# One fp32 matmul per span on a half of TensorE's columns, in batches, in place of three fp32r matmuls

## The chip, the cores and the metric

The kernel runs on one core of one Trainium2 chip. What counts is the time of one execution on the device, in microseconds: the median of three runs.

## What is computed

One layer of a mixer for a prompt of 1024 tokens and for one new token of each of 8 samples. The parts that matter here are the attention outputs of the prompt, cut to their core:

```python
def nsa_core(...):                  # for a block of queries
    ...                             # o_c: attention over compressed keys; imp: importance of blocks
    _, idx = lax.top_k(imp, n_sel)  # blocks of 64 keys that a query selects
    s_s = jnp.where(m_s, s_s, NEG)  # scores of the selected keys, causal
    p_s = jax.nn.softmax(s_s, axis=-1)
    o_s = jnp.einsum('bqgrnl,bgqnld->bqgrd', p_s, v_sel)
    ...
    p_w = jax.nn.softmax(jnp.where(m_w, s_w, NEG), axis=-1)   # the last 512 keys
    o_w = jnp.einsum('bqgrk,bkgd->bqgrd', p_w, vw)
    return o_c, o_s, o_w

o_a = gw[..., 0] * o_c + gw[..., 1] * o_s + gw[..., 2] * o_w  # gates by query and head
```

There are 8 query heads in 2 groups; the 4 heads of a group share keys and values of 64 channels. Everything else (modulation, projections, the spatial mix, gates, merge, output projection) surrounds this.

## The kernel before

The work comes in stages: modulation and projections of the tokens (to some 250 us of the profiled span), attention of the samples (to 410 us), attention of the prompt (some 415 to 822 us), merge and output projection (to the end). Beside the attention of the samples and of the prompt run channel-major projections as filler: `stream(jobs)`, whose matmuls write `mm` banks. A job has three pieces (344 columns each) of 24 matmuls; `paced()` lets the jobs last as long as the attention and keeps a rest of them, PACE_REST pieces, for the time after it.

All order is fixed when the program is made. Each stream of work is a Python generator; `Plan` estimates when each engine gets to what has been emitted, from a cost for each operation, and `Plan.go` always takes the next step of the stream that would make PE wait least. The result is one list of instructions for each engine, which the engine works off in order, with semaphores where one engine needs what another made. A wrong estimate changes the order, not what is computed.

Most matmuls are fp32r, one pass; a number is split into a high and a low half where more precision is needed, and three products of halves are added up. A matmul on plain fp32 operands is also possible; it shows in the trace as two instructions.

The attention of the prompt goes over 16 tiles (`TILES`: two groups, eight tiles of 128 queries each). `front` prepares a tile's queries, the compressed branch, the selection and the maxima of the scores. A tile has spans (`spans(i)`): pairs of a branch (1 the window, 0 the chosen blocks) and a tile of 128 keys, 2 to 13 of them, 132 in all 16 tiles. For each span:

- `scores` makes the scores, keys by (head, query), 128 x 512, with two matmuls into an `st` bank, and `pt` = exp of them on ScalarE; on the diagonal and at the window's far edge GpSimd sets entries to zero (`affine_select`, 40 of them). There are four `pt` buffers.
- `low` makes the halves of p: `p2[:, 0]` by a copy on ScalarE or (each third span) VectorE, `p2[:, 1]` by a subtraction on VectorE or (each third) GpSimd.
- `outputs` has three matmuls for it into a `pv` bank. `vv` holds, for each tile of keys, [v_hi, ones, v_lo] of 64 columns each, so the first and the third have 128 columns, of which 64 give the sums of p, and the second has 64 columns:

```python
pe.matmul(x, lhsT=v[:, 0:128], rhs=p2[:, 0], start=first, ...)
pe.matmul(x[0:64], lhsT=v[:, 128:192], rhs=p2[:, 0], start=False, ...)
pe.matmul(x, lhsT=v[:, 0:128], rhs=p2[:, 1], start=False, ...)
```

The window's spans come first and fill one bank, then the chosen ones fill another. When a branch is done, `weigh` copies the row of sums (`sr`) and the outputs (`u`) out of the bank on ScalarE and spreads the sums over partitions by a DMA (`s8`). When both are done, `close` forms the weights gate / sum, sends them through DRAM (`w_d`) to be spread over partitions (`f`), multiplies `u` by them on GpSimd, adds the compressed branch (two matmuls, `vc4` by `pgT`) and stores the tile. Closing the last tile of a group lets what depends on it go on; closing the last of all ends the stage. DMAs are issued from SP's queue, in order.

In the profile nearly every instruction has the line L217, that of the helper that records operations, so groups are told apart by their tiles: `pv<-p,vv` are the output matmuls, `p<-pt` and `p<-pt,p` the halves, `u`, `sr`, `s`, `f` what `weigh` and `close` handle, `mm<-hh,c0h` and the like the jobs, `mm<-araw,cT` the fp32 matmuls of the modulation (9 x 512), `mx<-plT,wck` another fp32 one.

Of the kernel before, what the change touches and what calls it, by code (L numbers as in the profile page):

```python
# [24 lines left out]
EPS = 1e-6  # L25
# [3 lines left out]
class Pack:  # L29
    """Constants that depend on the shapes alone, as columns of one [128, n] array."""  # L30
# [62 lines left out]
class Plan:  # L93
    """Estimates when the engines get to what has been emitted, so that independent streams of work can be
    emitted in an order in which the engines wait little. It has no part in what is computed."""
# [35 lines left out]
    def meet(x, y):  # L131
        """Whether two accesses to a tile, as box() gives them, overlap."""
# [8 lines left out]
    def after(self, ap, writes_only, engine=None):  # L141
        """When the accesses to the elements of ap are over."""
# [117 lines left out]
def nsa_gmlp_step(ctx: ExitStack, tc: tile.TileContext, a: dict):  # L260
# [46 lines left out]
    def rows(name, n, m=128):  # L307
        """The n elements of an input on each of m partitions."""
# [38 lines left out]
    def rsqrt(out, x, scale, n, p=128):  # L347
        """out = (x * scale + EPS) ** -0.5"""
# [24 lines left out]
    def weights(todo):  # L373
        """Loads slices (key, source, columns) in order and cuts them into hi and lo, but for those used as they are."""
# [46 lines left out]
    def x_turned(first):  # L421
        """RMS-normalised x, transposed: every other tile."""
# [26 lines left out]
    def x_loads():  # L449
        """The tiles of x behind the weights of the modulation, which all wait for."""  # L450
# [38 lines left out]
    def modulation():  # L489
        """Shift and scale of the samples and the prompt (column 8), and from them h."""  # L490
# [54 lines left out]
    def h_split():  # L545
        """h as its halves, as it comes."""
# [27 lines left out]
    def rope_tab(which):  # L574
        """[cos * g | sin * g'] so that rope(x * g) = x * cos_g + swap(x) * sin_g"""
# [9 lines left out]
    def constants():  # L585
        """What P1 needs beside its weights, each in time."""
# [25 lines left out]
    def fold(i, p, n):  # L612
        """The rows of the hi and lo halves of the samples, added."""
# [12 lines left out]
    def norm_rope(p, m, i, nh, t, final, done, x=None):  # L626
        """rope(rms_norm(p) * g) into the parts of final: (first head, end, out)"""
# [85 lines left out]
    def gate_rows():  # L713
        """The gate rows of the modulation, to DRAM until the end."""
# [137 lines left out]
    class Chunk:  # L852
        """128 columns of a weight as hi and lo [128, k, 128]."""
# [17 lines left out]
    def paced():  # L871
        """Whether the jobs are not ahead of the attention, so that they last as long as it does."""
# [8 lines left out]
    SPANS, PACE_LEAD, PACE_FRONT, PACE_REST = 132, 12, 14, 6  # L881
# [18 lines left out]
    def stream(jobs):  # L900
        """Jobs of (source of weights, body, condition): the weights of the next job load while this one runs."""
# [24 lines left out]
    def gate_tanh(p, n):  # L926
        """tanh(p / 2), so that p * sigmoid(p) = p * (1 + tanh(p / 2)) / 2"""
# [24 lines left out]
    def z_body(br, c):  # L952
        """silu(z) of a branch, times x where that is there, to DRAM until the merge."""
# [13 lines left out]
    def products(br):  # L967
        """What the projection of a branch takes, as its halves."""
# [23 lines left out]
    def gate_job(br, c):  # L992
        """tanh of half the merge gates of 128 channels, to DRAM until the merge."""
# [14 lines left out]
    def merge_job(br, j):  # L1008
        """Two chunks of 128 channels of a branch in model width, times the gate: all of m, or added to it."""
# [44 lines left out]
    def hand_over():  # L1054
        """When the rotary parts are done, their space goes to the weights of the jobs."""
# [50 lines left out]
    def decode():  # L1106
# [3 lines left out]
        def gather(name, s):  # L1110
            """Rows of sample s: partition p holds its tokens 8p..8p+7."""
# [5 lines left out]
        def window(src, dst, newrow, s):  # L1117
            """The last 511 cached rows and the new one: partition p holds rows 4p..4p+3."""
# [17 lines left out]
        def window_out(what, s):  # L1136
            """The window of a sample when it is loaded; it goes to its output."""
# [19 lines left out]
        def windows():  # L1157
            """The windows in turn, each when there is room, so that the other loads don't wait behind it."""
# [16 lines left out]
        # queries [hi | lo], by sample in zero-padded columns  # L1175
# [21 lines left out]
        # gates by (sample, head)  # L1197
# [9 lines left out]
        # compressed rows and key scores  # L1207
# [51 lines left out]
        def window_keys():  # L1259
            """Scores of the window and the compressed values, beside the selection."""  # L1260
# [19 lines left out]
        # compressed keys  # L1280
# [13 lines left out]
        def fold2(out, b):  # L1294
            """Rows of the hi and lo queries, added."""
# [3 lines left out]
        def softmax(x, mcol, gcol):  # L1299
            """Raw scores to probabilities, times the gate if there is one"""  # L1300
# [34 lines left out]
        # scores of the selected blocks and the new row  # L1335
# [14 lines left out]
        def turn_p(x, n, name):  # L1350
            """Probabilities [64, n*128] to [128, n, hi 64 | lo 64]"""
# [34 lines left out]
        # values of the selected and window rows, two samples at a time  # L1386
# [49 lines left out]
        for par in range(2):  # L1436
# [12 lines left out]
    areg = region("a", "right")  # L1449
    TILES = [(0, i) for i in (1, 2, 3, 4, 0, 5, 6, 7)] + [(1, i) for i in (2, 3, 4, 5, 6, 1, 7, 0)]  # L1450
    L1, L2, vv = ({(g, w): areg.tile(shape, FR, name=f"{n}{g}{w}") for g, w in ((0, 0), (0, 1), (1, 0))}
                  for n, shape in (("L1", [128, T]), ("L2", [96, T]), ("vv", [128, 8, 192])))
    for x in (L1, L2, vv):
        x[1, 1] = x[0, 1]
    PT_BUFS, P_BUFS = 4, 4
# [3 lines left out]
    one = areg.tile([128, 64], F32, name="one")  # L1459
# [14 lines left out]
    def g_load(j):  # L1474
        """Gates of a tile by (branch, head, token), eight on a partition."""
# [8 lines left out]
    def prepare():  # L1484
        for n in range(2):
            k_load(n)
        for n in range(PT_BUFS):
            e_load()
# [37 lines left out]
    def blocks():  # L1526
        """The rows of L2 that take the maxima to the keys of their blocks."""
# [6 lines left out]
    def keys():  # L1534
        """L1 = [k_hi; k_hi], L2 = [k_lo; blocks] and [v_hi | v_lo] of the branches of the groups, three at a time."""
        for g, w in ((0, 1), (0, 0), (1, 0), (1, 1)):
# [24 lines left out]
            for hf in range(2):  # L1561
# [12 lines left out]
    def spans(i):  # L1574
        """Key tiles of query tile i: (branch, tile), those of the window first."""
        return [(1, k) for k in range(max(0, i - 4), i + 1)] + [(0, k) for k in range(i + 1)]

    def front(g, i):
        """Queries, compressed branch, selection and the score maxima of tile i."""
# [26 lines left out]
        def maxima(w, flat, c, width, dst):  # L1606
            """Row maxima over runs of `width` keys, four (head, key tile) pairs at a time."""
# [96 lines left out]
    def scores():  # L1704
        """Scores by keys and their exponentials, ahead of the outputs."""
        for g, i in TILES:
# [4 lines left out]
            for n, (w, k) in enumerate(spans(i)):  # L1711
# [13 lines left out]
                plan.add(low(g, i, n, pt), 0)  # L1725
            scored[0] += 1

    def low(g, i, n, pt):
        """The halves of the probabilities of a span."""
        yield pt  # L1730
        yield lambda: flying[0] < P_BUFS
        flying[0] += 1
# [10 lines left out]
    def outputs():  # L1743
        """Outputs of the branches, a span at a time."""
        for g, i in TILES:
            o, x, todo = {}, None, spans(i)
            for n, (w, k) in enumerate(todo):
                yield lambda: (g, i, n) in cut and (g, w, "v") in built
                p2 = cut.pop((g, i, n))
                first = n == 0 or todo[n - 1][0] != w  # L1750
                if first:
                    yield lambda: open_[0] < 2
# [270 lines left out]
```

## Time and profile before

| | |
|---|---|
| median of 3 runs | 1042.09 us (1040.89 to 1042.28) |
| span of the profiled execution | 1039.6 us |
| PE (matmuls) busy | 1018.3 us, 98% |
| VectorE, ScalarE, GpSimd busy | 657.1, 468.5, 305.5 us |
| attention of the prompt, 440 to 825 us: PE busy | 379.7 us |

The span goes from the first to the last instruction of one profiled execution; the median is of other executions, from outside, and is some 2.5 us longer. Busy times are unions of the drawn instructions of an engine. The drawn length of a matmul includes the way out of the array, so matmuls overlap in the drawing, and the distance between starts is what one costs.

### The profile page before, as it was taken

Reading aid. Unit: us, or ns where it says so; the run is one execution under the profiler, and the core shown is the slowest. Engines: PE = TensorE matmul, PEld = TensorE weight load, DVE = VectorE, ACT = ScalarE, POOL = GpSimd, SP = SyncE. Lnnn points to the kernel's source line nnn. Section 1 sums busy time; section 2 is a strip of 40 time slices with the busy share of each in tenths; the row PEclk is TensorE's granted clock in tenths of the full one; section 3 lists DMA queues with packets and bytes.
Section 4 is the critical chain, followed back from the end, with each engine's and each line's share of the span. In section 5 each row is a group of like instructions: output and inputs, shape, how many; then the busy total and the mean of one; then the engine's idle time right before and its main releaser. Section 6 shows DMA issues by size and latency. Waiting matters only on the chain. (4 is left out here: it accounts for less than half of the span.)

```text
span 1039.6 us, 16376 instructions
## 1 busy us (share of the span) xinstructions
PE 1018.3 (98%) x5747; PEld 878.7 (85%) x5747; DVE 657.1 (63%) x1372; ACT 468.5 (45%) x984; POOL 305.5 (29%) x332
## 2 busy tenths in 40 slices
PE   7999999999999999999999999999999999999998
PEld 2589977879999999987878788778788999998776
DVE  5676786354668766578787868895753147675322
ACT  5763332001332244767766677677666242232000
POOL 0453565454221110013334332433333100251000
PEclk9999999999999999999999999999999999999999
DMA  9735451103875745521212121211111478554321
GB/s 328 263 95 175 135 185 52 61 22 129 277 213 149 256 152 192 151 67 41 79 53 72 35 64 49 68 38 51 50 58 59 126 248 254 187 163 146 120 91 62
DMA packets 106311, 130.33 MB, mean 125 GB/s; under 512 B 27299, under 2 KB 71525, under 8 KB 106230
## 3 DMA queue, kind: packets, MB, share of 16 engines
q1 hardware_dynamic: 101622, 112.52, 33.7%
q0 software_dynamic: 4608, 16.78, 5.2%
q8 instruction: 45, 0.74, 0.3%
q14 instruction: 36, 0.29, 0.1%
HBM read 98.95 MB, written 30.23 MB: 124 GB/s over the span
## 5 line engine op out<-in xcount | busy, mean ns | idle before, releaser
L217 PE MATMUL pv<-p,vv 128*128 128x512 f32 (+1 forms) x396 | 111.7, 399 | 0.5 <-DVE p L217 0.4
L217 PE MATMUL mm<-hh,c0h 128*128 128x344 f32 x320 | 105.3, 329 | 0.0
L217 ACT ACTIVATE pt<-st 128x512 f32<-128x512 f32 x132 | 78.7, 596 | 58.5 <-PE st L217 56.1
L217 PE MATMUL mm<-hh,c1h 128*128 128x344 f32 x320 | 104.9, 328 | 0.0
L217 PE MATMUL mm<-hl,c0h 128*128 128x344 f32 x320 | 102.3, 320 | 0.0
L217 PE MATMUL mm<-hl,c1h 128*128 128x344 f32 x320 | 102.2, 319 | 0.0
L217 PE MATMUL mm<-hh,c1l 128*128 128x344 f32 x320 | 102.2, 319 | 0.0
L217 PE MATMUL mm<-hh,c0l 128*128 128x344 f32 x320 | 102.2, 319 | 0.0
L217 PE MATMUL st<-R,L 128*128 128x512 f32 (+1 forms) x264 | 88.2, 415 | 0.0
L217 PEld LDWEIGHTS pv<-p,vv 128*128 128x128 f32 (+1 forms) x396 | 65.7, 172 | 22.4 <-DVE p L217 1.9
L217 DVE TENSOR_TENSOR p<-pt,p 128x512 fp32r<-128x512 f32 x88 | 69.4, 794 | 17.7 <-ACT p L217 17.1
L217 POOL TENSOR_TENSOR p<-pt,p 128x512 fp32r<-128x512 f32 x44 | 60.0, 1364 | 53.9 <-ACT p L217 53.9
L217 ACT ACTIVATE p<-pt 128x512 fp32r<-128x512 f32 x94 | 59.1, 629 | 13.6 <-POOL pt L217 12.3
L217 POOL TENSOR_SCALAR_AFFINE_SELECT pt<-pt 128x512 f32<-128x512 f32 x40 | 29.3, 732 | 121.7 <-ACT pt L217 119.8
L217 PE MATMUL mx<-L,R 128*128 128x512 f32 (+3 forms) x204 | 61.7, 364 | 1.8 <-DVE bm L217 1.1
L217 PEld LDWEIGHTS mm<-hh,c1h 128*128 128x128 f32 x320 | 60.3, 188 | 2.9 <-issue 0.2
L217 PEld LDWEIGHTS mm<-hh,c0h 128*128 128x128 f32 x320 | 60.4, 189 | 2.5 <-issue 0.2
L217 PEld LDWEIGHTS mm<-hh,c1l 128*128 128x128 f32 x320 | 60.3, 188 | 2.5
L217 PEld LDWEIGHTS mm<-hh,c0l 128*128 128x128 f32 x320 | 60.3, 188 | 2.1
L217 PEld LDWEIGHTS mm<-hl,c0h 128*128 128x128 f32 x320 | 60.1, 188 | 0.0
L217 PEld LDWEIGHTS mm<-hl,c1h 128*128 128x128 f32 x320 | 60.1, 188 | 0.0
L217 ACT ACTIVATE th<-mm 128x344 f32<-128x344 f32 x68 | 30.9, 454 | 58.3 <-PE mm L217 58.0
(497 smaller groups left out, 2669.3 us busy)
## 6 DMA issues: line engine op xcount, KB each, us to landing
t_db<-th SPq DMA_DIRECT2D x24, 172.0 KB
t_da<-th SPq DMA_DIRECT2D x24, 172.0 KB
th<-t_db SPq DMA_DIRECT2D x24, 172.0 KB
th<-t_da SPq DMA_DIRECT2D x24, 172.0 KB
graw<-in_w_ada_dram SPq DMA_DIRECT2D x16, 256.0 KB
araw<-in_w_ada_dram SPq DMA_DIRECT2D x16, 256.0 KB
xt<-in_x_dram SPq DMA_DIRECT2D x8, 512.0 KB
eraw<-in_w_ada_dram SPq DMA_DIRECT2D x16, 256.0 KB
```

The source lines that it names most:

```text
L217: r = getattr(real, name)(*args, **kw)
```

## The change

Each span's output becomes one matmul of plain fp32, v (64 columns) by `pt` (512 columns), with no halves and no ones. Both branches share a bank: the window's output on partitions 64 to 127, the chosen's on 0 to 63, that is, on two halves of the array's columns. `spans` alternates the branches as long as both have spans, and `outputs` emits a tile's matmuls in batches of at most eight, when all of a batch's `pt` are there (tiles of 2, 4, 6 and 8 spans in one batch; of 10, 11, 12 and 13 in 6+4, 6+5, 6+6 and 8+5). `pt` gets 14 buffers.

The sums of p are made apart: `total` (in place of `low`) adds up the `pt` of a branch, on GpSimd for two of three spans and on VectorE for the third, and `sum_up` takes the sum over the 128 keys with four small fp32 matmuls of a column of ones, 32 columns by 256, on the four quarters of the array's columns. It is emitted in front of the next tile's first batch (for the last tile, at the end). `sum_row` copies the result and spreads it with four DMAs a tile, where `weigh` had one a branch. Some numbers change with it: U_TILES 3 instead of 2, PACE_REST 12 instead of 6, and the planner takes a plain fp32 matmul of up to 64 columns for half as long as it did. Comments are dropped.

```diff
@@ Plan.cost
-                cost, passes = max(4 * n / 2.4, 208 * m / 128), 4
+                cost, passes = max(4 * n / 2.4 / (2 if m <= 64 else 1), 208 * m / 128), 4
@@
-    SPANS, PACE_LEAD, PACE_FRONT, PACE_REST = 132, 12, 14, 6
+    SPANS, PACE_LEAD, PACE_FRONT, PACE_REST = 132, 12, 14, 12
@@
-                  for n, shape in (("L1", [128, T]), ("L2", [96, T]), ("vv", [128, 8, 192])))
+                  for n, shape, dt in (("L1", [128, T], FR), ("L2", [96, T], FR), ("vv", [128, 8, 64], F32)))
-    PT_BUFS, P_BUFS = 4, 4
+    PT_BUFS, BATCH = 14, 8
-    one = areg.tile([128, 64], F32, name="one")
+    one = areg.tile([128, 32], F32, name="one")
@@ keys
-                v = v8[:, 4 * hf:4 * hf + 4]
-                split(v[:, :, 0:64], v[:, :, 128:192], v4)
-                act.activation(v[:, :, 64:128], one[:, None, :].to_broadcast([128, 4, 64]), AF.Copy)
+                act.activation(v8[:, 4 * hf:4 * hf + 4], v4, AF.Copy)
@@ spans
-        return [(1, k) for k in range(max(0, i - 4), i + 1)] + [(0, k) for k in range(i + 1)]
+        window, chosen = [(1, k) for k in range(max(0, i - 4), i + 1)], [(0, k) for k in range(i + 1)]
+        return [x for two in zip(window, chosen) for x in two] + chosen[len(window):]
@@ low, now total
-        p2 = areg.tile([128, 2, 512], FR, name="p2", bufs=P_BUFS)
-        if n % 3 in HI_DVE:
-            dve.tensor_copy(p2[:, 0], pt)
+        key = g, i, w
+        if key not in sums:
+            sums[key] = pt
         else:
-            act.activation(p2[:, 0], pt, AF.Copy)
-        yield p2[:, 0]
-        (pool if n % 3 in ON_POOL else dve).tensor_tensor(p2[:, 1], pt, p2[:, 0].bitcast(F32), op=OP.subtract)
-        waiting[0] -= 1
-        cut[g, i, n] = p2
+            old = sums[key]
+            if key not in added:
+                added.add(key)
+                sums[key] = areg.tile([128, 512], F32, name="acc", bufs=4)
+            (pool if n % 3 in ON_POOL else dve).tensor_tensor(sums[key], old, pt, op=OP.add)
+        cut[g, i, n] = pt
@@ outputs
+            x = bank("pv")
+            n_batches = -(-len(todo) // BATCH)
+            size = -(-len(todo) // (2 * n_batches)) * 2
+            for n0 in range(0, len(todo), size):
+                some = range(n0, min(n0 + size, len(todo)))
+                yield lambda: all((g, i, n) in cut for n in some) and (g, 0, "v") in built and (g, 1, "v") in built
+                pts = [cut.pop((g, i, n)) for n in some]
+                yield pts[-1]
+                if due:
+                    yield from sum_up(*due.pop())
+                for n, pt in zip(some, pts):
+                    w, k = todo[n]
+                    pe.matmul(x[64 * w:64 * w + 64], lhsT=vv[g, w][:, k, :], rhs=pt, start=n < 2, stop=False, skip_group_check=True)
+                    spanned[0] += 1
+                waiting[0] -= len(some)
                 yield 0
@@ sum_up
+        b = bank("mx")
+        for h in range(2):
+            for w in range(2):
+                at = 64 * w + 32 * h
+                pe.matmul(b[at:at + 32, 0:256], lhsT=one, rhs=sums[g, i, w][:, 256 * h:256 * h + 256], start=True, stop=True)
@@ sum_row
+        act.activation(sr, b[:, 0:256], AF.Copy)
+        s8s[j] = areg.tile([128, 8], F32, name="s8", bufs=U_TILES)
+        for n in range(4):
+            dma(s8s[j][32 * n:32 * n + 32], sr[32 * n:32 * n + 1])
@@
-    ON_POOL = (1,)
-    HI_DVE = (2,)
+    ON_POOL = (1, 2)
-    U_TILES, s8s = 2, {}
+    U_TILES, s8s = 3, {}
```

`weigh` now copies both branches' `u` out of the one bank, and `close` also waits for the tile's `s8`.

## Rows read from the trace of the kernel before

**Rows 1.** The page: busy time by engine, PE in 40 slices, and the granted clock.
```profile
PE 1018.3 (98%) x5747; PEld 878.7 (85%) x5747; DVE 657.1 (63%) x1372; ACT 468.5 (45%) x984; POOL 305.5 (29%) x332
PE   7999999999999999999999999999999999999998
...
PEclk9999999999999999999999999999999999999999
```

**Rows 2.** Busy time by stretch: from:to, length, each engine's busy time (instructions), clock, DMA.
```profile
core 0: us, PE busy (x) PEld busy (x) DVE busy (x) ACT busy (x) POOL busy (x), PEclk, DMA share, GB/s
0.00:60.00 60.00, 52.34 (x225) 27.37 (x225) 39.02 (x86) 39.85 (x79) 19.07 (x32) 1.00 0.78 271
...
440.00:825.00 385.00, 379.67 (x2172) 320.31 (x2173) 269.13 (x595) 258.30 (x550) 130.54 (x147) 1.00 0.20 60
```

**Rows 3.** Who waited for whom, 440 to 825 us: total, times, longest.
```profile
POOL pt L217 <- ACT pt L217: 119.8, 33, 13.1
...
POOL u L217 <- DMA f<-w_d: 33.8, 10, 7.4
...
PEld pv L217 <- DVE p L217: 1.9, 4, 0.9
```

**Rows 4.** PE's groups of instructions, shapes apart: busy us, mean ns, idle before.
```profile
L217 PE MATMUL pv<-p,vv 128*128 128x512 f32 x264 | 102.3, 402 | 0.5 <-DVE p L217 0.4
...
L217 PE MATMUL pv<-p,vv 128*64 128x512 f32 x132 | 51.9, 393 | 0.0
```

**Rows 5.** The timeline of PE around 713 us: start, length, merged instructions.
```profile
712.99 0.39 PE L217 MATMUL st<-R,L 96*128 96x512 f32 x1
713.22 1.55 PE L217 MATMUL pv<-p,vv 128*128 128x512 f32 x6
714.61 0.62 PE L217 MATMUL st<-R,L 128*128 128x512 f32 x2
```

**Rows 6.** The timeline of PE at the first and the last output matmuls.
```profile
455.04 0.94 PE L217 MATMUL pv<-p,vv 128*128 128x512 f32 x3
455.82 0.32 PE L217 MATMUL mm<-hh,c1h 128*128 128x344 f32 x1
...
804.73 0.86 PE L217 MATMUL pv<-p,vv 128*128 128x512 f32 x3
805.43 0.32 PE L217 MATMUL mm<-hh,c0h 128*128 128x344 f32 x1
```

**Rows 7.** The timeline of PE at fp32 matmuls of the modulation.
```profile
26.89 1.02 PE L217 MATMUL mm<-graw,cT 128*9 128x512 f32 x2
27.75 0.59 PE L217 MATMUL mm<-araw,cT 128*9 128x512 f32 x1
```

**Rows 8.** The timeline at an fp32 matmul of 128 columns by 256.
```profile
308.03 0.59 PE L217 MATMUL mx<-plT,wck 128*128 128x256 f32 x2
```

**Rows 9.** Groups of instructions of the other engines, 440 to 825 us.
```profile
L217 DVE TENSOR_TENSOR p<-pt,p 128x512 fp32r<-128x512 f32 x88 | 69.4, 794 | 17.7 <-ACT p L217 17.1
...
L217 POOL TENSOR_TENSOR p<-pt,p 128x512 fp32r<-128x512 f32 x44 | 60.0, 1364 | 53.9 <-ACT p L217 53.9
L217 ACT ACTIVATE p<-pt 128x512 fp32r<-128x512 f32 x94 | 59.1, 629 | 13.6 <-POOL pt L217 12.3 <-PE pv L217 0.2
...
L217 DVE CAST p<-pt 128x512 fp32r<-128x512 f32 x38 | 21.6, 568 | 10.2 <-ACT pt L217 10.2
```

**Rows 10.** Instructions on the tiles sr and u: duration least/median/most, first and last start.
```profile
L217 SPq DMA_DIRECT2D s<-sr x32: 469/494/565, 465.4 to 806.4; - x32
...
L217 DVE TENSOR_TENSOR u<-mx,u x16: 406/424/425, 488.8 to 822.7; 128x256 f32<-128x256 f32 x16
```

**Rows 11.** The chain that ended last, in order of time, after the last output matmul.
```profile
805.60 7.55 PE mm L217 x48
```

More of the change, by code (lines that the diff above doesn't have):

```diff
@@ L1450, in nsa_gmlp_step @@
     TILES = [(0, i) for i in (1, 2, 3, 4, 0, 5, 6, 7)] + [(1, i) for i in (2, 3, 4, 5, 6, 1, 7, 0)]
-    L1, L2, vv = ({(g, w): areg.tile(shape, FR, name=f"{n}{g}{w}") for g, w in ((0, 0), (0, 1), (1, 0))}
-                  for n, shape in (("L1", [128, T]), ("L2", [96, T]), ("vv", [128, 8, 192])))
+    L1, L2, vv = ({(g, w): areg.tile(shape, dt, name=f"{n}{g}{w}") for g, w in ((0, 0), (0, 1), (1, 0))}
+                  for n, shape, dt in (("L1", [128, T], FR), ("L2", [96, T], FR), ("vv", [128, 8, 64], F32)))
     for x in (L1, L2, vv):
         x[1, 1] = x[0, 1]
-    PT_BUFS, P_BUFS = 4, 4
+    PT_BUFS, BATCH = 14, 8
     BT = [areg.tile([128, 4, 32], F32, name=f"BT{n}") for n in range(2)]
@@ L1743, in outputs @@
     def outputs():
+        due = []
         for g, i in TILES:
[L1746 to L1752, printed above, removed]
-                    open_[0] += 1
-                    x = bank("pv")
-                yield p2[:, 1]
-                v = vv[g, w][:, k, :]
-                pe.matmul(x, lhsT=v[:, 0:128], rhs=p2[:, 0], start=first, stop=False, skip_group_check=True)
-                pe.matmul(x[0:64], lhsT=v[:, 128:192], rhs=p2[:, 0], start=False, stop=False, skip_group_check=True)
-                pe.matmul(x, lhsT=v[:, 0:128], rhs=p2[:, 1], start=False, stop=False, skip_group_check=True)
-                flying[0] -= 1
-                spanned[0] += 1
-                if n + 1 == len(todo) or todo[n + 1][0] != w:
-                    part.add((g, i, w))
-                    plan.add(weigh(g, i, w, x, o), 0)
-                yield 0
@@ L1766, in outputs @@
[L1766 to L1773 removed]
+            todo = spans(i)
+            yield lambda: open_[0] < 2
+            open_[0] += 1
+            x = bank("pv")
[13 more added lines that the diff above has]
+                waiting[0] -= len(some)
+                yield 0
@@ new lines, in outputs, with sum_up @@
+            for w in range(2):
+                part.add((g, i, w))
+            o = {}
+            due.append((g, i))
+            plan.add(weigh(g, i, x, o), 0)
+            plan.add(close(g, i, pgTs.pop((g, i)), o), 0)
+        yield from sum_up(*due.pop())
+    def sum_up(g, i):
+        yield sums[g, i, 0]
+        yield from free_bank("mx")
+        b = bank("mx")
+        for h in range(2):
+            for w in range(2):
+                at = 64 * w + 32 * h
+                pe.matmul(b[at:at + 32, 0:256], lhsT=one, rhs=sums[g, i, w][:, 256 * h:256 * h + 256], start=True, stop=True)
+        for w in range(2):
+            del sums[g, i, w]
+        plan.add(sum_row(TILES.index((g, i)), b), 0)
@@ L1775, in weigh, with sum_row @@
+    def sum_row(j, b):
+        yield b
+        sr = areg.tile([128, 256], F32, name="sr", bufs=2)
+        act.activation(sr, b[:, 0:256], AF.Copy)
+        s8s[j] = areg.tile([128, 8], F32, name="s8", bufs=U_TILES)
+        for n in range(4):
+            dma(s8s[j][32 * n:32 * n + 32], sr[32 * n:32 * n + 1])
+    ON_POOL = (1, 2)
+    pgTs, cut, sums, added = {}, {}, {}, set()
+    waiting, scored, open_ = [0], [0], [0]
+    def weigh(g, i, x, o):
         j = TILES.index((g, i))
@@ L1777, in weigh @@
         yield lambda: tiles[1] > j - U_TILES
-        u = areg.tile([128, 2, 128], F32, name="u", bufs=2 * U_TILES)
-        sr = areg.tile([65, 512], F32, name="sr", bufs=2)
-        act.activation(sr[64:65], x[64:65], AF.Copy)
-        if j not in s8s:
-            s8s[j] = areg.tile([128, 8], F32, name="s8", bufs=U_TILES)
-        dma(s8s[j][64 * w:64 * w + 64], sr[64:65])
-        x = x.rearrange("p (c a q) -> p c a q", c=2, a=2)
-        for par in range(2):
-            act.activation(u[64 * par:64 * par + 64], x[0:64, :, par, :], AF.Copy)
+        us = [areg.tile([128, 2, 128], F32, name="u", bufs=2 * U_TILES) for _ in range(2)]
+        for w, u in enumerate(us):
+            xw = x[64 * w:64 * w + 64].rearrange("p (c a q) -> p c a q", c=2, a=2)
+            for par in range(2):
+                act.activation(u[64 * par:64 * par + 64], xw[:, :, par, :], AF.Copy)
         open_[0] -= 1
-        o[w] = u
-    U_TILES, s8s = 2, {}
+        o.update(enumerate(us))
+    U_TILES, s8s = 3, {}
     w_d = [spill(f"w_d{j}", [128, 8]) for j in range(2 * NT)]
@@ L1795, in close @@
         j = TILES.index((g, i))
-        yield lambda: len(o) == 2 and tiles[2] == j
+        yield lambda: len(o) == 2 and tiles[2] == j and j in s8s
         tiles[2] += 1
```

10 lines of the change are left out of this document (2 added, 8 removed).

## The prediction

> **What bounds the kernel now.** I read the busy times of the page first: TensorE matmuls fill 98% of the span, VectorE 63%, ScalarE 45%, GpSimd 29%, and the granted clock is at its upper level of 2.4 GHz in all 40 slices [rows 1]. Then the busy time by stage: in the attention, 440 to 825 us, PE is busy 379.7 of 385 us, VectorE 269, ScalarE 258, GpSimd 131 [rows 2]. A busy PE could still be a PE whose matmuls wait inside, so the next view is who waited for whom in that stage: the weight loads of the output matmuls waited 1.9 us in all for p, in 4 places, though VectorE, ScalarE and GpSimd wait tens of microseconds for each other and for DMAs [rows 3]. The stage is bound by the sum of PE's work; the channel jobs (`mm`) fill every hole that attention leaves. So a change there is worth what it takes from PE's time or adds to it, and what it does to the other engines counts only where PE comes to wait for them.
>
> The drawn length of a matmul (393 to 402 ns here [rows 4]) includes its way out of the array; the price is the distance between starts. Six output matmuls take 1.39 us from 713.22 to the next start at 714.61, 232 ns each [rows 5]. From the timeline, the distance from each of the 396 to the next matmul's start adds up to 97.1 us (first at 455.04, last ending with the start at 805.43 [rows 6]): 92 us of streaming and 5 us of small waits.
>
> **What it removes from PE.** All 396 of those matmuls, three for each of 132 spans: 97.1 us.
>
> **What it adds to PE, one.** For each span one full fp32 matmul of 64 x 512. No fp32 matmul with a span's shape is in the trace. The nearest is that of the modulation, 9 x 512: it shows as two instructions, which begin at 26.89 and, with the next matmul, at 27.75, 0.86 us for the two; over all 32 of the kind the median distance of starts is 0.434 an instruction, 0.868 for two [rows 7]. The one of 128 columns by 256 takes 0.215 an instruction (0.59 drawn for two, 0.375 for one) [rows 8]. The price goes with the 512 streamed columns and not with the width, so 132 spans would cost 132 x 0.868 = 114.6 us if each had the array alone.
>
> The gain hangs on two of them running side by side: the window branch goes to partitions 64 to 127 of the bank, the chosen branch to 0 to 63, and `spans` now alternates them. No row shows two matmuls at once. One end of the bound is none of it, 114.6 us. The other is perfect pairing: 30 pairs a group, and 6 spans of the chosen branch without a partner, 36 x 0.868 x 2 groups = 62.5 us. I take a value between, for a reason in the rows: the 5747 starts on PE are in program order, and the two instructions of an fp32 matmul stand next to each other, on the same half. Take a slot of 0.434 us. In the first slot runs A1 alone; then A2 beside B1; then B2 beside the next span's C1; at the end the last one alone. A batch of n alternating spans takes n + 1 slots, a span without a partner two more. Tiles of 2, 4, 6, 8, 10, 11, 12 and 13 spans, in batches of 2, 4, 6, 8, 6+4, 6+5, 6+6 and 8+5, take 3, 5, 7, 9, 12, 14, 16 and 18 slots: 84 a group, 168 in all, **72.9 us**. Two streams at once draw 1024 columns in 0.434 us, 2.36 a nanosecond; the fp32r matmul of the rows draws 512 in 232 ns, 2.2. If that were a limit of reading, the 96 shared slots would take 0.464 and the sum 2.9 us more; I take 0.434, which both fp32 rows show, and keep 2.9 for the range.
>
> **Two.** The sums: 16 times four fp32 matmuls of 32 x 256 on four quarters, eight instructions of 0.215. In order and by halves as above: A1, A2+B1, B2+C1, C2+D1, D2, five slots, 1.075 us, 16 times **17.2 us**. Its ends: all four at once, two slots, 6.9 us; none at once, 27.5 us.
>
> **Three.** Changes between whole array, halves and quarters: 24 batches and 16 sums, 64 changes. The rows show such a change: the middle matmul of each old span has 64 columns and stands between two of 128 [rows 4], and six in a row with four such changes inside still take 232 ns each [rows 5]. I price them at nothing. The Trainium skill, *TensorEngine Tiling (Array Packing)*, section Key Properties, says that a change of tiling mode drains TensorE. By that rule each change would cost about what a drawn matmul is longer than its stride; this trace doesn't agree, as far as a lone narrow matmul tells. The waits at the head of a batch or a sum I take as 40 times 0.05 us (the first old span took 0.78 for three instead of 0.70 [rows 6]), 2 us, between 0 and 5.
>
> **The sum.** 72.9 + 17.2 + 2 - 97.1 = -5.0 us. The profiled span is 1039.6 us, 2.5 us below the median of 1042.09, so 1034.6 in the span and **1037** in the measured time.
>
> **What lies beside PE.** Removed: 94 copies of p on ScalarE (59.1 us), 38 casts and 88 subtractions on VectorE (21.6 and 69.4), 44 subtractions on GpSimd (60.0) [rows 9]. Added: 100 additions of p, by n mod 3 66 on GpSimd at 1.36 us (90 us) and 34 on VectorE at 0.79 (27). GpSimd goes from 131 to some 160 of 385 us [rows 2], still the idlest. All at nothing, and so are the copies of v that go: PE hides them. The row of sums goes out by 64 DMAs instead of 32, at 0.49 us of issue each [rows 10], 16 us more of SP's queue; behind it stand weight loads and the stores of the jobs. A job lasts three pieces of 24 x 0.157 us (48 take 7.55 [rows 11]), 11 us, and its weights load a job ahead, which covers it.
>
> The sum now waits for the last addition, and is taken in front of the next tile's first batch, so `close` of a tile comes a tile later; U_TILES 3 and five pgT make room. After the last output matmul 17.3 us pass until the last `u` at 822.7 [rows 6, 10]; these are covered by jobs. The chain grows by the sum and its copy, 2 us or so, and PACE_REST 12 keeps 12 pieces (45 us) instead of 6 (23 us) for it. Nothing, but without that cover the 17.3 us would be bare. The planner's new cost for narrow fp32 also reaches the 16 modulation matmuls; there loads set the pace (DMA 0.78, PE 52.3 of 60 us [rows 2]), so nothing, at most 2 us either way.
>
> **Rivals.**
> *Free pairing.* The halves don't wait for each other's order, and four quarters run at once: 62.5 + 6.9 + 2 - 97.1 = -25.7, 1016 us. For it: nothing in the rows forbids it; against it: the order of starts. The Trainium skill, *TensorE: Matmul & The Clock Gate*, section The mechanism, has matmuls start and end strictly in program order and only weight loads pulled ahead; that is the forecast's order, and this trace's starts agree.
> *No pairing*, the change doesn't do what it says: 114.6 + 27.5 + 2 - 97.1 = +47, 1089 us. It is slower from the point where a span costs over 0.59 us on average ((97.1 - 17.2 - 2) / 132) instead of 0.55. For it: no row shows two at once. Against it: a 64-column matmul takes as long as a 128-column one [rows 4], so half of the columns lie idle, and one fp32 instruction streams at half the rate of the fp32r one.
> *A batch waits for GpSimd.* A batch needs its last pt, which on the diagonal passes `affine_select` on GpSimd; in that queue stand the products of `close`, which waited for their DMA 10 times, 33.8 us, up to 7.4 [rows 3]. All spans of the batch and every job behind it on PE then wait. Against it: today's output matmuls depend on the same queue and waited 1.9 us. If four batches meet a wait of 3.4 us, +13.5 on the forecast: 1050. It turns the sign from two such waits on.
> *Drains.* 64 changes at 399 - 232 = 0.167 us [rows 4, 5]: +10.7, 1048 us.
>
> **How the numbers follow.** Order by halves (the forecast) 0.50, its own range 1032 to 1043 (paired slots, waits, planner); free pairing 0.24; no pairing 0.10; GpSimd 0.10; drains 0.04; the rest 0.02. A measurement of this kernel can tell about 0.2%, 2.1 us, from no change. The forecast's case falls below that in 7 of 10, above none: faster 0.24 + 0.35 + 0.01 = 0.60, same 0.14, slower 0.26. The range takes in free pairing and half of the GpSimd case, 1013 to 1050; it leaves out no pairing and the rest, under 0.2.
>
> **What would show it.** In the trace after: 264 fp32 output instructions whose starts within a batch come two by two, or 0.217 us apart on average; the last of a batch alone; a batch of 8 in 3.9 us (3.5 if pairing is free, 6.9 if there is none); sums in 1.1 us. PE's waits for `pt` or `acc` stay under 5 us. The forecast is wrong if starts stand 0.43 us apart throughout, if batches begin with microseconds of idle PE, or if fewer jobs run beside attention so that PE runs dry before the merge.

## The result: slower, with less work on TensorE

The changed kernel takes 1071.02 us, the kernel before 1042.18 us beside it: a ratio of 1.0279 [1.0258, 1.03]. The profiled span goes from 1039.6 to 1066.4 us, 26.8 more. The forecast was 1037, between 1013 and 1050.

From the page of the changed kernel: busy time by engine, PE in 40 slices, granted clock. It answers [rows 1].

```profile
PE 1022.6 (96%) x5743; PEld 840.6 (79%) x5743; DVE 602.4 (56%) x1272; ACT 396.9 (37%) x866; POOL 330.2 (31%) x354
...
PE   7999999999999999999999998899899799999998
...
PEclk9999999999999999999999998999999899999999
```

Busy time by stretch in the changed kernel: from:to, length, each engine's busy time (instructions), clock, DMA. It answers [rows 2].

```profile
440.00:835.00 395.00, 369.19 (x2099) 268.59 (x2098) 215.20 (x498) 186.24 (x432) 153.34 (x169) 0.98 0.19 56
835.00:1066.00 231.00, 226.49 (x1230) 205.00 (x1228) 106.14 (x184) 46.60 (x80) 25.84 (x25) 0.99 0.50 154
```

Where PE had no hole before, there are slices of 70 and 80% in the attention and two below full clock. PE is idle for 26 of 395 us, where it was for 5 of 385 [rows 2]. VectorE and ScalarE have less to do, as forecast (215 instead of 269 us, 186 instead of 258), and nothing comes of it.

The same by stages, from the first and last starts of their instructions, in us:

| | before | after |
|---|---|---|
| up to the first split of the attention's queries | 423.3 | 427.6 |
| from there to the last `u` | 399.8 | 408.3 |
| last `u` to the merge's first matmul | 23.9 | 37.9 |
| merge | 91.5 | 91.3 |
| output projection, to the end | 101.1 | 101.1 |

So 4.3 us come ahead of the stage, 8.5 in it and 14 between it and the merge, where 9.7 pieces of jobs run instead of 6.3 (233 matmuls instead of 151), since PACE_REST holds more of them back.

What became of PE's time in the same 385 us, 440 to 825, is worked out from the distances of starts, each kind of matmul taken at its steady stride (the 344-column job matmul at 0.157 us, a pair of output matmuls at 0.434). The last column is the kernel of the experiment "three undone", below:

| us of 385 | before | after | three undone |
|---|---|---|---|
| streaming at the steady stride | 361.8 | 325.1 | 340.1 |
| of it jobs | 148.8 | 133.2 | 150.1 |
| entering and leaving groups of narrow matmuls | 0 | 7.9 | 17.4 |
| gaps of over 0.5 us | 4.8 | 21.4 | 6.2 |
| lost to the half clock | 0 | 6.9 | 0 |
| smaller gaps | 18.1 | 23.4 | 21.2 |

The work of the outputs did fall, and by more than was forecast. It was replaced by gaps, not by jobs: 15.6 us fewer of those ran in this time. PACE_REST has a part in that: 929 job matmuls are drawn in this time before and 832 after, but 940 in the changed kernel with PACE_REST 6, below.

The waits of 440 to 850 us in the changed kernel, who for whom: total, times, longest. They answer [rows 3].

```profile
POOL acc L217 <- ACT pt L217: 94.6, 30, 18.0
...
PEld pv L217 <- issue: 35.1, 114, 0.4
...
DVE s L217 <- DMA s<-sr: 22.8, 8, 5.4
...
POOL u L217 <- DMA f<-w_d: 19.7, 7, 13.7
...
PEld mx L217 <- DVE bm L217: 9.7, 16, 1.3
...
PE mx L217 <- DVE bm L217: 7.9, 15, 1.3
...
PE mx L217 <- DVE u L217: 6.1, 1, 6.1
```

PE's waits are not at the output matmuls, which is where the forecast looked for them. They are at `mx`, the bank of the selection, the maxima and the closing, for VectorE to empty it (`bm`, `u`). "issue" before `pv` is the load that comes when its half is free; it is the pace of the pairs and not a wait.

Last, how the stage ends: the chain that ended last in the changed kernel, in order of time: start, length, what.

```profile
811.74 3.58 PE pv L217 x10
815.32 0.67 PE st L217 x2
815.99 0.95 PE mx L217 x9
...
818.15 0.39 ACT sr L217
...
818.56 0.57 SPq L217
...
822.34 0.59 SPq L217
...
822.97 3.00 DMA s<-sr
...
827.62 3.33 DMA f<-w_d
...
831.12 1.40 POOL u L217 x2
...
833.36 0.44 DVE u L217
833.84 6.25 PE mx L217 x24
```

In the kernel before, this chain held nothing but matmuls [rows 11]. Now it passes through the last sums: eight DMA issues on SP (818.56 to 822.92), the landing of `s`, that of `f`, two products, and only then a job that was given an `mx` bank. PE's timeline at that place (start, length, instructions, idle before):

```profile
827.40 0.32 PE L217 MATMUL mm<-hl,c0h 128*128 128x344 f32 x1
833.84 0.66 PE L217 MATMUL mx<-hh,c0h 128*128 128x344 f32 x1 [6.11 <-DVE u L217]
834.29 0.49 PE L217 MATMUL mx<-hh,c0l 128*128 128x344 f32 x1
...
838.59 0.39 PE L217 MATMUL mx<-hh,c0l 128*128 128x344 f32 x1
838.82 0.32 PE L217 MATMUL mx<-hl,c0h 128*128 128x344 f32 x1
```

After 6.1 us of waiting the matmuls are drawn 0.49 us long instead of 0.32 and start 0.287 us apart instead of 0.157, until 838.8: the clock's lower level, 1.2 GHz. The records show it four times in and right behind this stage (647.6 to 654.4, 671.5 to 674.9, 756.8 to 760.2, 831.9 to 838.7 us, 20.5 us in all, of which at most half is lost). The last falls within the wait of 6.1 us, the others stand right behind or between waits of 0.4 to 1.7 us. Two waits of that size at 624 us (0.66 and 0.59) had no such stretch behind them. The kernel before has none in the stage [rows 1].

### The profile page after: what moved, and what is told of

Same layout as the page of the kernel before. It is cut to its first block, busy times and chain, and to the rows that moved or that the text cites. A ratio compares the mean times of both kernels' runs of the same rounds, so it can differ in the third digit from the quotient of the medians.

```text
span 1066.4 us, 16209 instructions
## 1 busy us (share of the span) xinstructions
PE 1022.6 (96%) x5743; PEld 840.6 (79%) x5743; DVE 602.4 (56%) x1272; ACT 396.9 (37%) x866; POOL 330.2 (31%) x354
## 5 line engine op out<-in xcount | busy, mean ns | idle before, releaser
L217 PE MATMUL mm<-hh,c1h 128*128 128x344 f32 x304 | 99.3, 327 | 0.0
L217 PE MATMUL mm<-hh,c1l 128*128 128x344 f32 x304 | 97.1, 319 | 0.0
L217 PE MATMUL mm<-hl,c1h 128*128 128x344 f32 x304 | 97.0, 319 | 0.0
L217 POOL TENSOR_TENSOR acc<-acc,pt 128x512 f32<-128x512 f32 x52 | 68.9, 1327 | 45.4 <-ACT pt L217 41.7
L217 PE MATMUL pv<-pt,vv 128*64 128x512 f32 x264 | 67.6, 601 | 0.0
L217 POOL TENSOR_TENSOR m<-m,th 128x344 f32<-128x344 f32 x24 | 25.3, 1078 | 108.9 <-DVE th L217 108.9
L217 DVE TENSOR_REDUCE bm<-mx 128x8 f32<-128x512 f32 x72 | 47.3, 684 | 12.3 <-PE mx L217 11.9
L217 PEld LDWEIGHTS mx<-L,R 128*128 128x128 f32 x204 | 40.1, 200 | 17.2 <-DVE bm L217 7.1
L217 PEld LDWEIGHTS st<-R,L 128*128 128x128 f32 (+1 forms) x264 | 43.4, 195 | 10.5 <-ACT pt L217 4.9
L217 DVE TENSOR_REDUCE wm<-mx 128x4 f32<-128x512 f32 x60 | 39.9, 686 | 17.0 <-PE mx L217 16.5
```

The costliest lines, as they stand in the source:

```text
L217: r = getattr(real, name)(*args, **kw)
```

## The experiments

Theory one: PE's sum doesn't bound the stage alone; fronts, additions, closings and their banks have a length of their own, and jobs only fill what they leave. Theory two: PE's sum does bound it, and the output matmuls cost more than was forecast. Theory three: the loss lies in the numbers that came along, PACE_REST and the planner's price. "Expected" texts stand as they were written before each run.

### Is the stage worth what PE's work is worth?

From the kernel before, the third output matmul of each span is dropped:

```diff
-                pe.matmul(x, lhsT=v[:, 0:128], rhs=p2[:, 1], ...)
```

> The kernel before without the third output matmul of each span (v times the low half of p is left out; the low half is still made). It takes 132 x 0.232 = 30.6 us from PE's work and touches nothing else. If attention is bound by the sum of PE's work, as the prediction had it: 1042 - 31 = 1011 us. If the stage has a length of its own (fronts, banks and the engines behind them), and the filler already only fills its holes: 1034 to 1042 us, with PE's waits in 440 to 825 us up by 20 us or more.

1034.63 us, 0.9934 [0.9918, 0.9951]. 132 matmuls of 0.232 us are 30.6 us of PE; 6.7 came out at the end. Its busy time by stretch, and PE's waits from 815 to 960 us:

```profile
440.00:825.00 385.00, 373.90 (x2181) 317.95 (x2180) 273.97 (x602) 259.82 (x562) 134.06 (x147) 1.00 0.23 66
825.00:1033.00 208.00, 192.04 (x996) 168.82 (x995) 100.85 (x175) 39.14 (x64) 24.90 (x24) 0.96 0.48 153
```

```profile
PE st L217 <- ACT xh L217: 9.7, 3, 6.3
```

The stage became 8.0 us shorter (391.8) and took in more jobs, so that only 10.7 us instead of 23.9 stood between the last `u` and the merge. But the merge reads what the last `u` has stored and loaded again, and waited for it: it took 105.2 us instead of 91.5, with 13.7 us of it at the lower clock. In that run's chain of waits the way goes from the last `u` (815.51) through its store (from 816.33, 1.68 us) and a load (from 819.54, 2.69 us) to `xh` at 822.24, and on through another load of 5.08 us. Up to the merge's first matmul 20.2 of the 30.6 us did come out (826.7 instead of 846.9); 13.7 of these were asked back behind. At the end a microsecond of PE was worth about a fifth of one, which ends the forecast's sum. The 20 us of waits in the stage that the expectation named with this outcome didn't come: PE was idle for 11.1 us of 385 instead of 5.3.

### How long is the stage without jobs?

In both kernels, no job runs before the last output matmul of the attention; all run behind it.

```diff
-        return pieces[0] - pace["at"] <= (pace["n"] - PACE_LEAD - PACE_REST) * done + PACE_LEAD
+        return False
```

> The kernel before with no job of the filler allowed beside the attention of the prompt: all of them run after it. The total time says nothing here; the length of the stage does, from the first query split to the last output of attention (399.8 us with filler). If the stage's own chain is nearly as long as the stage, as the run with two products of three says: 320 to 350 us, with PE idle or waiting in a good part of it. If PE's work alone made the length: PE's attention work without jobs, about 220 us.

> The changed kernel with the same edit. If the change makes the stage's own chain longer though it takes work from PE (batches that wait for eight spans, sums that wait for additions): 10 to 25 us longer than the kernel before alone. If the length follows PE's work: 17 to 22 us shorter.

1159.56 and 1188.49 us, one execution each and so without an interval. From the first split to the last `u` it takes 360.3 us in the kernel before and 383.7 in the changed one. Busy time by stretch, first of before, then of the changed kernel:

```profile
420.00:780.00 360.00, 297.90 (x1328) 201.30 (x1329) 258.95 (x581) 240.61 (x515) 130.22 (x145) 0.89 0.12 29
```

```profile
420.00:780.00 360.00, 290.71 (x1229) 157.15 (x1231) 198.62 (x478) 164.80 (x389) 142.54 (x158) 0.81 0.11 29
```

Without jobs PE is busy 298 of 360 us, part of it at half clock, and no other engine comes near its limit: the stage is a chain of hand-overs. It is longer than the 320 to 350 us expected, with 76.5 us of it at the lower clock. With the jobs beside it (925 matmuls more, some 145 us at 0.157) it takes 399.8, 39.5 more. So the 98% of [rows 1] was in good part jobs in holes.

The changed kernel's stage without jobs is 23 us longer, as expected, but the pair doesn't show that its chain of hand-overs is. The second line ends 32 us before that stage does; over each whole stage PE is idle for 60.0 us before and 67.7 after, and busy for 300.3 and 316.0, with 76.5 and 135.2 us at the lower clock. So 7.7 of the 23 us are idle time, and the 58.7 us more at the lower clock can account for the rest.

### Do two halves run side by side?

The changed kernel with the old order of the spans, window then chosen; a batch is still of eight.

```diff
-        return [x for two in zip(window, chosen) for x in two] + chosen[len(window):]
+        return window + chosen
...
-                    pe.matmul(..., start=n < 2, ...)
+                    pe.matmul(..., start=n == 0 or todo[n - 1][0] != w, ...)
```

> The changed kernel with the old order of spans, the window's first and then the chosen ones, so that neighbouring output matmuls go to the same half of the columns; everything else alike. If two output matmuls run side by side only as neighbours on different halves: starts 0.43 us apart instead of two by two, about 50 us more output work on PE, 1090 to 1120 us. If the two instructions of one fp32 matmul were what runs side by side: starts as now, 1062 to 1075 us.

1096.84 us, 1.052 [1.0497, 1.0542], 26 above the changed kernel. The output matmuls take 98.7 us of PE from start to start, against 65.9. A batch of eight spans in the changed kernel, from PE's timeline:

```profile
628.35 0.64 PE L217 MATMUL mx<-acc,one 128*32 128x256 f32 x8
628.92 3.65 PE L217 MATMUL pv<-pt,vv 128*64 128x512 f32 x16
632.50 0.74 PE L217 MATMUL st<-R,L 128*128 128x512 f32 x2
```

Sixteen instructions take 3.58 us to the next start: eight steps of 0.43 and 0.15 beside them. They begin two by two, 5 to 7 ns apart (628.921 and 628.927, 629.402 and 629.407). The same number with the old order, whose weight loads show how they go:

```profile
642.18 0.19 PEld L217 LDWEIGHTS pv<-pt,vv 128*64 128x64 f32 x2 [0.41 <-issue]
642.67 0.14 PEld L217 LDWEIGHTS pv<-pt,vv 128*64 128x64 f32 x1 [0.29 <-issue]
...
644.38 0.14 PEld L217 LDWEIGHTS pv<-pt,vv 128*64 128x64 f32 x1 [0.29 <-issue]
644.81 0.19 PEld L217 LDWEIGHTS pv<-pt,vv 128*64 128x64 f32 x3 [0.29 <-issue]
645.24 0.19 PEld L217 LDWEIGHTS pv<-pt,vv 128*64 128x64 f32 x2 [0.23 <-issue]
645.67 0.19 PEld L217 LDWEIGHTS pv<-pt,vv 128*64 128x64 f32 x2 [0.23 <-issue]
646.16 0.14 PEld L217 LDWEIGHTS pv<-pt,vv 128*64 128x64 f32 x1 [0.29 <-issue]
```

One load each 0.43 us, then two trains at once from 644.81. The matmuls' starts split into ten in steps of 0.43 (642.187 to 646.100) and six (644.818 to 647.015): five window spans and three chosen ones, two instructions each (the records don't name the span; this is the only division that leaves each half one instruction at a time). The first chosen one begins while three instructions of window spans, emitted before it, are still to come. On different halves a matmul doesn't wait for those ahead of it, but here it got only three instructions ahead; for all of them to run in pairs, neighbours in the program had to lie on different halves.

### What does a batch cost?

```diff
-    PT_BUFS, BATCH = 14, 8
+    PT_BUFS, BATCH = 14, 2
```

> The changed kernel with batches of two spans (66 batches instead of 24), everything else alike. If long uninterrupted batches are what makes PE wait later (what feeds VectorE and ScalarE stands still for 3.5 us): about 1052 us. If the changes between the whole array and its halves cost most of the loss: 42 more batches at 0.25 us or more each, 1082 us or above.

1063.58 us, 1.0216 [1.0199, 1.0233]: 7.4 us faster than the changed kernel, with 66 batches instead of 24. One of them, PE's timeline:

```profile
617.48 1.08 PE L217 MATMUL pv<-pt,vv 128*64 128x512 f32 x4
618.49 0.74 PE L217 MATMUL st<-R,L 128*128 128x512 f32 x2
```

1.01 us for two steps of 0.43: 0.15 more, and the job matmul ahead of a batch takes 0.09 longer to the next start than its stride. The excess hardly depends on the size: batches of 4, 8, 12 and 16 instructions take 1.009, 1.867, 2.726 and 3.584 us in the changed kernel, 0.429 a step. Taken at the forecast's 0.434, 24 batches and 16 sums are 62.5 + 24 x 0.14 = 65.9 and 6.9 + 16 x 0.14 = 9.1 us, which is what was measured. So batches of two cost PE 42 x 0.23, some 10 us more, and the kernel is faster all the same: another time that PE's sum is not what counts.

The result lies between the two that were expected. The first output comes 30.0 instead of 38.6 us after the split (31.7 before), and the stage takes 403.0 instead of 408.3 us. But PE's waits for `bm` fell too (4.7 instead of 7.9 us), and so did the time at the lower clock in and behind the stage (10.2 instead of 20.5 us); which of these made the 7.4 us the run doesn't tell.

### What do the additions cost?

The changed kernel with only the first addition of a branch and tile; the rest of the sum is left out.

```diff
                 sums[key] = areg.tile([128, 512], F32, name="acc", bufs=4)
-            (pool if n % 3 in ON_POOL else dve).tensor_tensor(sums[key], old, pt, op=OP.add)
+                (pool if n % 3 in ON_POOL else dve).tensor_tensor(sums[key], old, pt, op=OP.add)
```

> The changed kernel with only the first addition of p for each branch of a tile (at most 30 of 100; the rest of the sum is left out). If the additions on GpSimd and VectorE are hidden, as the prediction priced them: 1071 us. If they lengthen the stage, because a tile's sum, weights and closing wait for them: about 1061 us, with attention 10 us shorter.

1057.26 us, 1.0155 [1.0129, 1.018]: 13.8 us less, with the same matmuls on PE. The stage takes 397.7 us. Leaving out additions gives back half of the loss, with the stage 10.6 us shorter, as the second expectation had it. Of the 72 left out 52 stood on GpSimd and 20 on VectorE, and the run doesn't separate them: GpSimd is busy 84.6 us of 440 to 825, and PE's waits for VectorE's `bm` fell from 7.9 to 2.2 us.

### PACE_REST

```diff
-    SPANS, PACE_LEAD, PACE_FRONT, PACE_REST = 132, 12, 14, 12
+    SPANS, PACE_LEAD, PACE_FRONT, PACE_REST = 132, 12, 14, 6
```

> The changed kernel with PACE_REST 6 as before. If the job pieces that PACE_REST 12 holds back are missing as filler beside attention and stand bare behind it: about 1062 us, with the time from the last output of attention to the first merge matmul back from 38 to some 25 us. If PE's work is simply conserved, wherever the pieces stand: 1071 us.

and the other way round in the kernel before:

> The kernel before with PACE_REST 12 alone. If held-back filler is lost as such: 1042 + 4 to 8 = 1048 us, attention shorter by some 8 us and the stretch to the first merge matmul longer by some 15. If the pieces are worth the same wherever they run: 1042 us.

Before with 12: 1051.1 us, 1.0084 [1.0068, 1.0099], so +9.6; the stage is as long as it was (399.4, where 8 us less were expected) and the distance to the merge is 33.9 instead of 23.9. The pieces that no longer run beside the attention leave holes there and stand bare behind it. The changed kernel with 6: 1067.29 us, 1.0253 [1.0236, 1.027], only 3.7 less. That was a miss. Its busy time behind the stage, and PE's waits from 845 to 960 us:

```profile
845.00:1061.00 216.00, 202.00 (x1058) 178.68 (x1056) 103.22 (x180) 41.17 (x69) 25.86 (x25) 0.97 0.50 155
```

```profile
PE st L217 <- ACT xh L217: 8.3, 3, 5.1
```

The distance to the merge fell by 27.5 us to 10.4, but the stage took 419.6 us (11.3 more) and the merge 104.0 instead of 91.3: as above, the merge waits for what the last `u` gives it. The held pieces have one use, to cover those some 20 us; more of them are bare, fewer show the wait.

### The planner's price

```diff
-                cost, passes = max(4 * n / 2.4 / (2 if m <= 64 else 1), 208 * m / 128), 4
+                cost, passes = max(4 * n / 2.4 / (2 if 32 <= m <= 64 else 1), 208 * m / 128), 4
```

The modulation (9 columns) is priced as before, the outputs and sums as in the change.

> The changed kernel with one number put back in part: the planner halves its price of a plain fp32 matmul only for 32 to 64 columns, so the modulation matmuls (9 columns) have their old price and only the attention keeps the new one. The stages ahead of attention take 4.3 us longer after the change than before. If that is the order that the new price makes there: the stages return to their old length, 1071 - 4 to 5 = 1066 us. If it is something else in the change (nothing else reaches those stages): 1071.

And in the kernel before, the new price alone:

> The kernel before with the planner's new price for narrow fp32 matmuls alone. If that price costs what the changed kernel gains without it: 1042 + 4 to 6 = 1047 us. If the price only matters together with the rest of the change: 1042 us.

1065.61 us, 1.0228 [1.0211, 1.0246], 5.4 less; and 1046.53 us, 1.0041 [1.0028, 1.0055], 5 more. The first split stands at 423.9 in the one and 426.6 in the other, against 427.6 and 423.3: most of it is lost ahead of the attention, since 16 matmuls that take 0.868 us and are thought to take half of it lead to another order there. The code of the kernel before with one wrong number shows it best: nothing that is computed has changed.

### All three undone

The changed kernel with the old price for the modulation, PACE_REST 6 and BATCH 2.

```diff
+                cost, passes = max(4 * n / 2.4 / (2 if 32 <= m <= 64 else 1), 208 * m / 128), 4
+    SPANS, PACE_LEAD, PACE_FRONT, PACE_REST = 132, 12, 14, 6
+    PT_BUFS, BATCH = 14, 2
```

> The changed kernel with three of its parts put back or cut: the old planner's price for the modulation, PACE_REST 6, batches of two. Alone these gave -5.4, -3.7 and -7.4 us. If they act in different places (order of the modulation, filler beside attention, the stage's chain): the sum, 1071 - 16 = 1054 us, perhaps 1046 if shorter attention also lets the filler fit. If they are one and the same slack counted three times: about 1062 us. It computes everything, so it may also stand against the kernel before (1042).

1042.95 us, 1.0015 [1.0004, 1.0026]. The whole loss is gone, and nothing is won. Busy time by stretch:

```profile
440.00:825.00 385.00, 379.11 (x2166) 269.34 (x2166) 215.83 (x493) 187.18 (x432) 152.11 (x163) 1.00 0.20 59
```

PE is as full as in [rows 2], at full clock, and the merge begins 17.5 us behind the last `u` and takes 92.5. The three gave 5.4, 3.7 and 7.4 us singly, 16.5 in all; together 28, more than either expectation. Of the 25.1 us between the two profiled spans 20.4 lie between the last `u` and the merge (17.5 instead of 37.9) and only 2.5 in the stage, which takes in 43.1 pieces instead of 38.0. The gaps of over 0.5 us fell from 21.4 to 6.2, and no time was spent at the lower clock, where it was 20.5 us. That the one brings the other, and that six pieces are enough because the stage ends early enough, is argued and not shown.

Why nothing is won stands in the table above: against the kernel before, 21.7 us less streaming meet 17.4 us of entering and leaving groups and 4.5 more in gaps. PE is full again, so this run alone would also fit theory two.

The last one takes the additions out as well, and leaves PACE_REST at 12:

```diff
+                cost, passes = max(4 * n / 2.4 / (2 if 32 <= m <= 64 else 1), 208 * m / 128), 4
+    PT_BUFS, BATCH = 14, 2
+                (pool if n % 3 in ON_POOL else dve).tensor_tensor(sums[key], old, pt, op=OP.add)
```

> The changed kernel with the old planner's price for the modulation, batches of two, and only the first addition of p for each branch of a tile (the rest of the sum is left out); PACE_REST 12. Alone -5.4, -7.4 and -13.8 us. If long batches and the additions are separate delays of the stage's chain: 1071 - 27 = 1044 us. If both stand in the same wait, and taking one makes the other free: 1052 to 1057 us.

1051.76 us, 1.0091 [1.0076, 1.0107], just below the second expectation. The stage takes 397.3 us, 8.5 less than with the additions, and the distance to the merge is 37.5 instead of 17.5. How much of the 8.5 is the additions and how much the six pieces that left the stage this pair doesn't tell (in the kernel before, moving them changed the stage by 0.4); what the stage gains goes to the bare pieces.

## Why the prediction was wrong

**The step that failed** is one sentence of its argument: "The stage is bound by the sum of PE's work". It was read from PE's 379.7 of 385 us and from output matmuls that hardly waited [rows 2, 3]. Both are true and don't say it. Jobs fill the holes, so PE's share is 98% whether the attention needs it or not: without jobs the stage still took 360.3 of its 399.8 us, and dropping 30.6 us of PE gave 6.7. With that step the forecast and the rival of free pairing fall together: both turn PE's sum into time.

**Removed, 97.1 us:** right.

**Added, order by halves, 72.9 us:** wrong in the harmless direction, 65.9. It rested on the starts being in program order; the three output matmuls of a span in the kernel before share columns, so its rows could show nothing else. The rival had it right: 62.5 us, and 3.4 for the batches' ends. With the old order of spans a chosen span's matmul began at 644.818 us, ahead of three instructions emitted before it. The rule of the Trainium skill that spoke for the forecast's order (*TensorE: Matmul & The Clock Gate*, section The mechanism: matmuls start and end strictly in program order) doesn't hold across halves here. The some 4 ns of issue overhead for each tile which the Trainium skill gives on that page, section Measured speedup vs the span model, are near the 5 to 7 ns measured between starts of neighbours.

**Sums, 17.2 us:** 9.1. All four quarters run at once, as in the rival.

**Changes of width, 0 plus 2 us for waits:** 7.9 us. Each of the 40 groups pays 0.14 in it, and 25 of them, those that follow the whole array, 0.09 ahead; the drains' rival (0.167 each, 10.7) was near. [rows 4, 5] misled: the lone 64-column fp32r matmul between two wide ones costs nothing, and was not the same thing. The rule of the Trainium skill, *TensorEngine Tiling (Array Packing)*, section Key Properties, that a change of tiling mode drains TensorE, agrees with the batches and not with that matmul.

**PE's work in all:** 62.5 + 6.9 + 7.9 - 97.1 = -19.8 us. The forecast said -5.0. It was wrong by 15 us there and by 34 at the end, the other way.

**Beside PE at nothing:** wrong. Without 72 of the 100 additions it is 13.8 us less. GpSimd's 160 of 385 us say little: an addition comes when its `pt` comes, in order, and GpSimd waited 94.6 us for them in all. That the sum, the closing and the next tile's banks come late behind the last addition is argued; VectorE, with 20 of those 72, may have emptied `mx` later because of them.

**Closing a tile later:** the chain from the last output matmul to the last `u` is as long as before, 17.5 us. That jobs cover it failed by a detail: the next piece of PE's list was due in an `mx` bank that the closing held, and all jobs stood behind it, 6.1 us and then 7 at the lower clock.

**PACE_REST as free cover:** wrong, 9.6 us in the kernel before. **The planner's price, at most 2 us:** wrong, 5. These two, small in the diff, make 14.6 us added up, half of the loss, each put alone into the kernel before; undone alone in the changed kernel they give 9.1.

**The rival of the wait for GpSimd** gave the right sign for the wrong reason. Batches didn't begin with idle PE; PE's matmuls waited 1.2 us for `pt`, under 5 as forecast. PE waited at `mx` instead. Of the forecast's signs of failure, the last one came true in its first half: fewer jobs ran beside the attention. PE then stood still for 6.1 us with pieces left, because the next one needed a held bank.

What stays open is how the time that the change adds splits between the first outputs' delay, the additions on either engine, the turns of the `mx` banks and the lower clock, and so why three reversals give more than their sum. The change with its batches of eight, but old price and old PACE_REST, wasn't run; nor were the additions on one engine alone left out. Nothing that was run is faster than the kernel before and computes the whole of it.

## What to carry to other kernels

An engine that is full because filler runs in its holes is not shown to be the bound: drop a known part of its work and see what comes out, before pricing a change by it, and look also at what stands behind the stage. When a change brings numbers with it (a reserve, a cost in a planner), undo each in turn, and put each alone into the kernel before; here these and the size of the batches make the difference between 28 us lost and none. Larger batches save changes of the array's width and can still cost more: here batches of two took some 10 us more of PE and the kernel was 7.4 us faster.

## What the runs showed of the hardware

- Two fp32 matmuls on 64 columns each ran fully side by side: 0.43 us for each of the two instructions that one of 512 columns has, on both halves at once. So did four of 32 columns by 256 (eight instructions in 0.57 us). Across halves starts left the order of the program, by three instructions.
- A group of narrow fp32 matmuls cost 0.23 us over its streaming when it stood between wide ones.
- In the changed kernel three stretches of 3 to 7 us at the lower clock began next to waits of PE of 0.4 to 1.7 us, a fourth within one of 6.1 us. They took at most 10 us, beside the waits themselves.
